# One activation for Silu, residual blocks by halves, and five changes of order in a two-layer encoder trunk

## The chip, the cores and the metric

The kernel runs on one core of a Trainium2 chip. The metric is the device time of one execution in microseconds (us), smaller being better; the median of a few runs is given with the lowest and the highest.

The engines are named as in the profile: PE (TensorE matmuls) and PEld (its weight loads), DVE (VectorE), ACT (ScalarE), POOL (GpSimd), SP (SyncE, which here only issues transfers). POOL issues transfers too.

## The reference

The input is a residual stream of 1024 tokens by 1024 features. Each of two layers computes, in float32:

```
h  = rmsnorm(x, g_mix);  p = h @ w_in
q  = rmsnorm(p[:384], g_q) @ w_uq          # 8 heads x (64 plain + 32 rotary)
kv = rmsnorm(p[384:640], g_kv) @ w_ukv     # 8 heads x (64 keys + 64 values)
k_rope = rope(p[640:672])
y_attn = softmax(q k^T / sqrt(96)) v
a, gt  = split(p[672:])
u  = a * sigmoid(gt)
u  = dwconv31(u) + b;  u = silu(layernorm(u))
x  = x + concat(y_attn, u) @ w_o
z  = dwconv3(rmsnorm(x, g_ffn) @ w_up) + b  # 2 x 2816 channels
zg, zv = split(z)
x  = x + (silu(zg) * zv) @ w_down
```

A last rmsnorm follows. silu(z) is z * sigmoid(z).

## The kernel before

Activations lie with features on the partitions and the 1024 tokens along the free axis; a block is 128 features by 1024 tokens in float32, and its halves are tokens 0 to 511 and 512 to 1023 (`HALVES`). Every matmul operand is carried as a high and a low part, both rounded to fp32r, and a product is three matmuls: high by high, high by low, low by high.

One layer goes through five stages.

**Projections** (`project`, matmuls on L210 and L479). They give the gate and value of the convolution, the query and key-value latents, the rotary parts and the queries. The gate's Sigmoid is on L532. A finished query block goes to DRAM (the spills `qd` and `qrd`), from where each head's rows are read back; the first head's rows are copied straight to its query tile `q`. The 31 taps of the convolution run on DVE (L1617) and, left over for the time of the attention, on ACT and POOL.

**Attention** (`attention`). A loop over n from -2 to 65 goes through 8 heads of 8 query tiles. One n makes the scores of tile n + 2 (six matmuls, L1438, into two PSUM banks `s`), the maximum (DVE, L1441), the exp of tile n + 1 (ACT, L1449), the transposes of tile n (L1465) with their casts `pt` on ACT (L1467) and DVE (L1468), and half of the values (L1489). `rows` (L1418) makes the values' operand for 128 tokens; `ROWS` says how many of them stand ahead of the first two scores. A table `agenda` runs further pieces after step n: the taps left over (`tap_late`, kinds `act`, `both` and `pool`: an `act` tap is one activation on L1633 and a transfer that adds it to the convolution), and the loads for the next stage. At the end `early(0, ...)` and `early(1, ...)` begin the output projection of the first two blocks.

**Output projection** (`wo_steps`, L835), with the norm of the convolution (`conv_norm`, L1652 to L1688), the residual in blocks `y`, and the second rmsnorm.

**Up projection** (`up_steps`). For each of 22 blocks f of channels seven products of half the size are made, in the order 1, 5, 6, 3, 7, 2, 4, each twelve matmuls of 128x512 (L1015). Products 1, 6, 7 and 4 go on accumulating in one bank, and 5 and 3 in another, so each of these waits until the one before it was evicted. An eviction is on ACT or on DVE (a copy or an add into `zg` or `zv`; the DVE ones on the helper line L964). The first 29 products, f from 0 to 3, have an order of their own (`START`). After them come the convolution of three taps (`o` from `zg`, `v` from `zv`; L1384 on ACT, L1390 on DVE), the Sigmoid (L1056) into a block `sg`, `gate` (o times sg) and `close` (v times o), and the store to DRAM (`act<-v`). Combined weights (`part`, `combine`, `cast`, `turn`: lines L964, L982, L1376, L1378 and L174) are made on DVE and ACT and partly added up by transfers that POOL issues.

**Down projection** (`down_steps`, L1207).

What sets the order: PE's, DVE's, ACT's and POOL's instructions keep the order in which the program writes them; SP's transfers are ordered by the framework's scheduler. In up, `put(step, rank, f)` puts a piece into the table of one step (a product is one step, 2.7 us), smaller ranks first. An eviction is put one step after its product at rank 0, unless `EVICT` names another step. The blocks share 31 buffers, so one is free again only when its last reader is done.

Of the kernel before, what the change touches and what calls it, by code (L numbers as in the profile page):

```python
# [16 lines left out]
T = 1024  # L17
# [45 lines left out]
LAST_MULT = (60, 61)  # L63
ROWS = (2, 4)
E = mybir.EngineType
# [10 lines left out]
LEFT = 4  # L76
# [8 lines left out]
ENDS = (slice(512, 768), slice(768, T))  # L85
EVICT = {(5, 0): 24, (5, 1): 25, (1, 2): 35, (1, 3): 36, (2, 2): 36, (2, 3): 37}
DOWN_ADDED = (2, 4)
# [23 lines left out]
class Encoder:  # L111
# [370 lines left out]
    def project(self, l, carry):  # L482
# [4 lines left out]
        gates, ckv, kvs, cq, cqs, vs, w = {}, [], [], [], [], [], {}  # L487
        heads, pending = {}, {}
        qd = [self.dp.tile([HEADS, NOPE, T], F32R, name=f"qd{l}{i}") for i in range(2)]
# [154 lines left out]
        def query_rope(i):  # L644
            p = ps[f"u{i}"]
            c, s = self.blk(f"rc{l}_{i}"), self.blk(f"rs{l}_{i}")
            nc.vector.tensor_tensor(out=c, in0=p, in1=st["cos"], op=ALU.mult)
            nc.vector.tensor_tensor(out=s, in0=p, in1=st["sin"], op=ALU.mult)
            st["rope", i] = c, s
            yield 2.44, 0.0  # L650
            if i == 0:
                return
            (c1, s1), (c2, s2) = st.pop(("rope", 0)), st.pop(("rope", 1))
            nc.vector.tensor_tensor(out=c1, in0=c1, in1=s2, op=ALU.subtract)
            nc.vector.tensor_tensor(out=c2, in0=c2, in1=s1, op=ALU.add)
            his = [self.blk(f"qr{l}_{i}", F32R) for i in range(2)]
            for hi, o in zip(his, (c1, c2)):
                nc.scalar.copy(out=hi, in_=o)
            yield 2.5, 1.0
            for i, (hi, o) in enumerate(zip(his, (c1, c2))):  # L660
                nc.vector.tensor_tensor(out=o.bitcast(F32R), in0=o, in1=hi.bitcast(F32), op=ALU.subtract)
                sp = hi, o.bitcast(F32R)
                yield 1.25, 0.0
                for p in range(2):
                    for h in range(DIRECT):
                        self.move(heads[h][0][p][NOPE + i * HALF:NOPE + (i + 1) * HALF, :],
                                  sp[p][h * HALF:(h + 1) * HALF, :])
                for p in range(2):
                    self.move(qrd[p][i].rearrange("h d t -> (h d) t"), sp[p], nc.gpsimd)

        def query(j):
# [112 lines left out]
    def layer(self, l, carry):  # L784
        with self.psum(f"mix{l}", ([f"w{i}" for i in range(3)], 1), 2):
            mixed = self.project(l, carry)
        with self.psum(f"attn{l}", 2, 4):
# [3 lines left out]
                     61: lambda: (ready.update({(1, 3): self.complete(*casts.pop(3))}), [casts.update({m: self.wo_cast(l, m, 1)}) for m in range(4, 8)])}  # L791
            begun = {"x": [], "po": {}}
            conv, ys = mixed[1], self.attention(l, *mixed, ahead, ready, begun)
# [43 lines left out]
    def wo_steps(self, l, conv, ys, w, casts, x, steps, put):  # L837
# [5 lines left out]
        def load_x():  # L843
            x.extend(self.load_y(l, m) for m in range(2, 8))

# [18 lines left out]
        def add_heads(c, m):  # L864
            xm = x[m][:, HALVES[c]]
            nc.vector.tensor_tensor(out=xm, in0=ps.pop((c, m)), in1=xm, op=ALU.add)

        def evict(c, m):
            xm = x[m][:, HALVES[c]]
            nc.vector.tensor_tensor(out=xm, in0=ps.pop((c, m)), in1=xm, op=ALU.add)  # L870
# [26 lines left out]
        def norm(c, k):  # L897
            xk = x[k][:, HALVES[c]]
            nc.vector.scalar_tensor_tensor(out=xk, in0=xk, scalar=par[:, P_GFFN + k:P_GFFN + k + 1], in1=rf[c],
                                           op0=ALU.mult, op1=ALU.mult)  # L900

        def first(k):
            norm(0, k)
            i = 1 + k // 4
            sets[i].append(self.pair(x[k][:, left], f"b{l}_{i}{k}", "m", True))

# [34 lines left out]
        put(18, 0.9, lambda: spread(1))  # L941
        b11, b12 = (lambda k, cs=cs: x[k][:, cs] for cs in HALVES)
        b21, b22 = (lambda k, cs=cs: x[k + 4][:, cs] for cs in HALVES)
        plan = ((5, 0, b11, b12, b11), (3, 4, b22, b22, None), (6, None, b11, b22, b11), (7, None, b12, b22, b12),
# [11 lines left out]
    def up_steps(self, l, steps, put):  # L956
# [95 lines left out]

        def sigmoid(f):
            z = st[f]
            z["s"] = self.blk(f"sg{l}_{f}")
            nc.scalar.activation(out=z["s"], in_=z["o"], func=AF.Sigmoid)  # L1056

        def gate(f):
            z = st[f]
            sub(z["o"], z["o"], z.pop("s"), ALU.mult)  # L1060

# [55 lines left out]
        for f in range(NF):  # L1117
# [288 lines left out]
    def attention(self, l, u, conv, away, spill, kvs, loaded, ahead, wo, begun):  # L1406
# [22 lines left out]
        def scores(n):  # L1429
# [4 lines left out]
            ps = self.wide(f"s{l}_{h}_{qt}")  # L1434
            for c in range(2):
                cs = slice(c * 512, (c + 1) * 512)
                for s, (i, j) in enumerate(((0, 0), (0, 1), (1, 0))):
                    nc.tensor.matmul(ps[:, cs], q[i][0:96, qs], k[j][0:96, cs],  # L1438
                                     start=(s == 0), stop=(s == 2))
            mx = self.cp.tile([128, 1], F32, name=f"mx{l}_{h}_{qt}", tag="mx", bufs=4)  # L1440
# [96 lines left out]
        def early_add(m):  # L1537
            xm = begun["x"][m][:, HALVES[0]]
            nc.vector.tensor_tensor(out=xm, in0=po[m], in1=xm, op=ALU.add)
# [21 lines left out]
        agenda[56].append(lambda: sums(last - 1, slice(0, 64), state[last - 1], state[last - 1]["y"], state[last - 1]["rb"]))  # L1561
        agenda[60].append(lambda: begun["x"].extend(self.load_y(l, m) for m in range(2)))
        for c, when in enumerate((60, 62)):
# [6 lines left out]
        for n in range(-2, total + 2):  # L1570
# [55 lines left out]
    def tap_late(self, l, j, t, u, y, kind):  # L1626
        lo, hi, s = self.span(t)
        p = self.blk(f"late{l}_{j}_{t}")
        if kind != "act":
            self.nc.gpsimd.tensor_tensor(out=p[:, lo:hi], in0=u[:, lo + s:hi + s],  # L1630
                                         in1=self.tap(l, j, t).broadcast_to([128, hi - lo]), op=ALU.mult)
        else:
            self.nc.scalar.activation(out=p[:, lo:hi], in_=u[:, lo + s:hi + s], func=AF.Copy, scale=self.tap(l, j, t))  # L1633
        if kind == "both":
# [10 lines left out]
    def conv_norm(self, l, conv, out, put):  # L1645
# [25 lines left out]
        def scale(j, c):  # L1671
            if (j, "z") not in st:
# [98 lines left out]
```

## Time and profile before

| | us |
|---|---|
| median of 3 runs | 2341.23 |
| lowest and highest | 2337.42, 2342.27 |
| the profiled execution | 2342.95 |
| its span | 2341.2 |

The span is that from the first to the last instruction of the profile; mean granted TensorE clock 0.995. Busy time is given by engine as a sum, a share of the span and a count of instructions. Busy shares are averages over stages of different kinds: a wait counts only where it is the last one to end in its stage. In a row of the timeline the brackets give how long the engine was idle ahead of it and which engine or transfer ended that.

### The profile page before, as it was taken

How to read it: one execution, taken by the hardware profiler on the slowest of the kernel's cores; microseconds unless marked ns; L12 is line 12 of the kernel's file. 1: busy time of each engine (PE TensorE's matmuls, PEld its weight loads, DVE VectorE, ACT ScalarE, POOL GpSimd, SP SyncE). 2: the span in 40 equal slices, each digit the busy share in tenths (PEclk: the TensorE clock that was granted, in tenths of full speed). 3: DMA queues.
4: the chain of work that ended last, by engine and by line, in shares of the span. 5: the costliest groups of instructions: out<-in, count | busy, mean ns of one | idle time of the engine just before them, and what ended most of it. 6: DMA issues, size and time to landing. Idle time of an engine off the chain costs nothing.

```text
span 2341.2 us, 31964 instructions
## 1 busy us (share of the span) xinstructions
PE 2298.8 (98%) x11256; PEld 1931.5 (83%) x11256; DVE 1787.9 (76%) x2404; ACT 1281.9 (55%) x2049; POOL 821.7 (35%) x837
## 2 busy tenths in 40 slices
PE   9999999999999999999999999999999999999997
PEld 7887899887788888888888888998877888888886
DVE  5987888768878787876559778887688787868665
ACT  5444877545755555544523467774465555555443
POOL 1222798613323323001412248964323332320032
PEclk9999999999999999999999999999999999999999
DMA  5887955936899998935968988547658999989366
GB/s 179 158 177 252 205 128 116 243 89 160 189 253 290 287 289 230 319 121 144 205 134 166 228 232 191 117 115 199 173 112 199 280 299 275 289 216 313 99 132 152
DMA packets 193969, 465.47 MB, mean 199 GB/s; under 512 B 26784, under 2 KB 34832, under 8 KB 193808
## 3 DMA queue, kind: packets, MB, share of 16 engines
q0 software_dynamic: 103712, 224.68, 46.3%
q1 hardware_dynamic: 90096, 238.74, 30.7%
q8 instruction: 89, 1.46, 0.3%
q14 instruction: 72, 0.59, 0.1%
HBM read 309.28 MB, written 80.40 MB: 166 GB/s over the span
## 4 chain that ended last, share of the span: by engine, by line
PE 78%; issue 6%; DVE 5%; DMA 4%; ACT 4%; POOL 2%; SPq 0%; POOLq 0%; ACTq 0%; DVEq 0%
PE p L1015 29%; PE pd L1207 14%; PE s L1438 6%; PE po L835 5%; PE o L1489 4%; PE t L1465 4%; PE pa L210 3%; PE pq L210 3%; PE pkv L210 2%; PE pg L210 2%; DMA w<-wu 1%; PE pg L479 1%; PE pk L210 1%; DVE wu L964 1%; PE pu L210 1%
## 5 line engine op out<-in xcount | busy, mean ns | idle before, releaser
L1015 PE MATMUL p<-b,w 128*128 128x512 f32 x3552 | 811.3, 390 | 8.8 <-DVE zg L964 3.3
L1015 PEld LDWEIGHTS p<-b,w 128*128 128x128 f32 x3552 | 666.6, 188 | 152.8 <-DVE zg L964 5.2
L1207 PE MATMUL pd<-ab,wd 128*128 128x512 f32 (+1 forms) x1920 | 422.3, 381 | 0.0
L1207 PEld LDWEIGHTS pd<-ab,wd 128*128 128x128 f32 x1920 | 350.7, 188 | 69.5 <-DVE ab L1378 0.4
L1438 PE MATMUL s<-k,q 96*128 96x512 f32 x768 | 208.9, 407 | 4.7 <-issue 1.9
L1468 DVE TENSOR_TENSOR pt<-t,pt 128x512 fp32r<-128x512 f32 x256 | 164.7, 684 | 60.8 <-ACT pt L1467 60.7
L175 POOL DMA_DIRECT2D w<-wu x96 | 84.1, 894 | 294.5 <-ACT w L174 265.2
L175 POOL DMA_DIRECT2D w<-in_w_up x116 | 100.9, 870 | 224.9 <-ACT w L174 210.7
L1467 ACT CAST pt<-t 128x512 fp32r<-128x512 f32 x256 | 137.5, 589 | 49.2 <-PE t L1465 43.1
L1630 POOL TENSOR_TENSOR late<-gate,par 128x1012 f32<-128x1012 f32 (+12 forms) x78 | 160.0, 2051 | 0.0
L1438 PEld LDWEIGHTS s<-k,q 96*128 96x128 f32 x768 | 134.8, 189 | 28.4 <-issue 3.8
L1441 DVE TENSOR_REDUCE mx<-s 128x1 f32<-128x1024 f32 x128 | 155.7, 1216 | 2.5 <-PE s L1438 2.5
L1489 PEld LDWEIGHTS o<-pt,v 128*128 128x128 f32 x1024 | 139.6, 190 | 13.7 <-issue 3.0
L1489 PE MATMUL o<-pt,v 128*128 128x256 f32 x1024 | 143.5, 283 | 2.8 <-DVE yt L1495 2.2
L964 DVE TENSOR_TENSOR zg<-p,zg 128x512 f32<-128x512 f32 x88 | 60.5, 690 | 111.5 <-PE p L1015 68.8
L1617 DVE SCALAR_TENSOR_TENSOR conv<-gate,par,conv 128x1009 f32<-128x1009 f32 (+7 forms) x112 | 142.3, 1274 | 3.6 <-ACT conv L541 1.0
L1449 ACT ACTIVATE p<-s,mx 128x1024 f32<-128x1024 f32 x128 | 144.9, 1132 | 0.0
L800 POOL DMA_DIRECT2D wd<-in_w_down x44 | 32.5, 741 | 310.9 <-PE pd L1207 308.8
L1465 PE MATMUL t<-ident,p 128*128 128x128 f32 x1024 | 133.6, 273 | 5.5 <-ACT p L1449 5.5
L1376 ACT CAST ab<-ac 128x512 fp32r<-128x512 f32 x130 | 80.1, 617 | 101.6 <-DVE ac L1142 99.1
L174 ACT ACTIVATE w<-w 128x512 fp32r<-128x512 f32 x212 | 133.5, 630 | 3.0
L1465 PEld LDWEIGHTS t<-ident,p 128*128 128x128 f32 x1024 | 114.4, 140 | 10.2 <-ACT p L1449 9.3
(2062 smaller groups left out, 4247.1 us busy)
## 6 DMA issues: line engine op xcount, KB each, us to landing
w<-in_w_up POOLq DMA_DIRECT2D x232, 256.0 KB, 6.5
wu<-in_w_up SPq DMA_DIRECT2D x88, 512.0 KB, 5.3
w<-wu POOLq DMA_DIRECT2D x96, 256.0 KB, 5.1
sd<-in_w_down SPq DMA_DIRECT2D x44, 512.0 KB, 9.8
ws<-sd SPq DMA_DIRECT2D x44, 512.0 KB, 6.3
wd<-in_w_down POOLq DMA_DIRECT2D x88, 256.0 KB, 5.3
act<-v SPq DMA_DIRECT2D x36, 512.0 KB, 5.9
ac<-act SPq DMA_DIRECT2D x72, 256.0 KB, 6.0
```

Of the source, the lines that this page charges most:

```text
L175: self.nc.gpsimd.dma_start(out=lo, in_=src, accum_op=ALU.add)
L210: nc.tensor.matmul(ps[:, HALVES[c]], w, x[:, HALVES[c]], start=(k == 0 and s == 0), stop=(k == n - 1 and s == 2))
L1015: nc.tensor.matmul(ps, w[p][:, k * 128:(k + 1) * 128], b[:, q], start=(i in (1, 5, 2) and k == 0 and t == 0), stop=(k == 3 and t == 2), sk ...
L1207: nc.tensor.matmul(ps[t, m][:, cs], w[i, j][p][:, m * 128:(m + 1) * 128], b[:, q, cs], start=(i in (1, 5, 2) and j == 0 and s == 0), stop= ...
L1438: nc.tensor.matmul(ps[:, cs], q[i][0:96, qs], k[j][0:96, cs], start=(s == 0), stop=(s == 2))
L1441: nc.vector.tensor_reduce(out=mx, in_=ps, op=ALU.max, axis=AX.X, negate=True)
L1449: nc.scalar.activation(out=p, in_=ps, func=AF.Exp, bias=mx, accum_out=st["sums"][:, qt:qt + 1])
L1465: nc.tensor.transpose(tp[:, i, :], p[:, kt * 128:(kt + 1) * 128], self.ident)
L1468: nc.vector.tensor_tensor(out=pt[1][g][:, :, qi * 128:(qi + 1) * 128], in0=tp, in1=hi.bitcast(F32), op=ALU.subtract)
L1489: nc.tensor.matmul(po, v[kt][:, h // 2, e, :], pt[s][kt // 4][:, kt % 4, :], start=(kt == 0 and s == 0), stop=(kt == 7 and s == 1))
L1617: self.nc.vector.scalar_tensor_tensor(out=y[:, lo:hi], in0=u[:, lo + s:hi + s], scalar=self.tap(l, j, t), in1=y[:, lo:hi], op0=ALU.mult, o ...
L1630: self.nc.gpsimd.tensor_tensor(out=p[:, lo:hi], in0=u[:, lo + s:hi + s], in1=self.tap(l, j, t).broadcast_to([128, hi - lo]), op=ALU.mult)
```

## The change

Seven things are changed.

1. **Silu.** The Sigmoid into `sg` and the product `gate` become one Silu activation in place, and so does the pair in the convolution's norm (there the add of the bias is in the activation). `close` of a block is put up to three steps earlier.
2. **Residual in halves.** `load_y` loads half blocks (128x512, blocks k and k + 4 of one half in a buffer) and first those of the first half.
3. **Query spills.** In `project` the spills of the queries are collected and written out after the next query.
4. **Taps on ACT** (`tap_late`, kind `act`) are two activations, one for each half, in two steps of the attention that hold no other such half; the adding transfer follows the second.
5. **Evictions in up.** `EVICT` names steps for (5,2), (5,3), (6,2), (6,3), (7,2), (7,3); its fraction is the rank.
6. **Scores** are made with the product of parts as the outer loop and the halves as the inner one.
7. **Order on PE in attention.** `ROWS` is (3, 4) for (2, 4): three `rows`, not two, ahead of the first scores, and one ahead of the second. Three of four parts of `early(1)` stand before the last values, behind `early(0)`.

The core of the diff:

```
-ROWS = (2, 4)
+ROWS = (3, 4)
...
-EVICT = {(5, 0): 24, (5, 1): 25, (1, 2): 35, (1, 3): 36, (2, 2): 36, (2, 3): 37}
+EVICT = {(5, 2): 30, (5, 3): 31, (6, 2): 38.295, (6, 3): 39.295, (7, 2): 40.295, (7, 3): 41.295, (5, 0): 24, (5, 1): 25, (1, 2): 35, (1, 3): 36, (2, 2): 36, (2, 3): 37}
...
-                for p in range(2):
-                    self.move(qrd[p][i].rearrange("h d t -> (h d) t"), sp[p], nc.gpsimd)
+                spills.extend((qrd[p][i].rearrange("h d t -> (h d) t"), sp[p]) for p in range(2))
...
-                self.move(qd[p][2 * j:2 * j + 2].rearrange("h d t -> (h d) t"), sp[p], nc.gpsimd)
+                spills.append((qd[p][2 * j:2 * j + 2].rearrange("h d t -> (h d) t"), sp[p]))
+            while j and spills:
+                self.move(*spills.pop(0), nc.gpsimd)
...
-    def load_y(self, l, m):
-        t = self.blk(f"y{l}_{m}")
-        self.nc.sync.dma_start(out=t, in_=self.xd[l][m])
-        return t
+    def load_y(self, l, x, c, k):
+        t = self.blk(f"y{l}_{c}{k}")
+        for e in range(2):
+            m = k + 4 * e
+            x[m, c] = t[:, HALVES[e]]
+            self.nc.sync.dma_start(out=x[m, c], in_=self.xd[l][m][:, HALVES[c]])
...
-        def sigmoid(f):
-            z = st[f]
-            z["s"] = self.blk(f"sg{l}_{f}")
-            nc.scalar.activation(out=z["s"], in_=z["o"], func=AF.Sigmoid)
-
-        def gate(f):
-            z = st[f]
-            sub(z["o"], z["o"], z.pop("s"), ALU.mult)
+        def silu(f):
+            o = st[f]["o"]
+            nc.scalar.activation(out=o, in_=o, func=AF.Silu)
...
-            put(EVICT.get((i, f), n + 1), 0, lambda i=i, f=f: evict(i, f))
+            m = EVICT.get((i, f), n + 1)
+            put(int(m), m % 1 * 10, lambda i=i, f=f: evict(i, f))
...
-            put(n + 3, 4, lambda f=f: sigmoid(f))
-            put(n + (7 if f >= LEFT else 5), 2.8, lambda f=f: gate(f))
+            put(n + 3, 4, lambda f=f: silu(f))
...
-            put(max(m + 3, n + (8 if f >= LEFT else 6)), 3, lambda f=f: close(f))
+            put(max(m + 3, n + 5), 3, lambda f=f: close(f))
...
-            for c in range(2):
-                cs = slice(c * 512, (c + 1) * 512)
-                for s, (i, j) in enumerate(((0, 0), (0, 1), (1, 0))):
-                    nc.tensor.matmul(ps[:, cs], q[i][0:96, qs], k[j][0:96, cs],
-                                     start=(s == 0), stop=(s == 2))
+            for s, (i, j) in enumerate(((0, 0), (0, 1), (1, 0))):
+                for cs in HALVES:
+                    nc.tensor.matmul(ps[:, cs], q[i][0:96, qs], k[j][0:96, cs], start=(s == 0), stop=(s == 2))
...
-        costs = [LATE_COST[kind] for kind in kinds]
+        costs, taken = [LATE_COST[kind] for kind in kinds], set()
         for i, (j, t) in enumerate(late):
-            agenda[int(SIDE_TIME * sum(costs[:i]) / sum(costs))].append(lambda i=i, j=j, t=t: self.tap_late(l, j, t, u[j], conv[j], kinds[i]))
+            n, steps = int(SIDE_TIME * sum(costs[:i]) / sum(costs)), self.tap_late(l, j, t, u[j], conv[j], kinds[i])
+            for e in range(2 if kinds[i] == "act" else 1):
+                while kinds[i] == "act" and n in taken:
+                    n += 1
+                if kinds[i] == "act":
+                    taken.add(n)
+                agenda[n].append(lambda steps=steps: next(steps, None))
+            if kinds[i] == "act":
+                agenda[n].append(lambda steps=steps: next(steps, None))
...
                 early(0, range(3))
+                early(1, range(3))
...
-        early(0, range(3, 4))
-        early(1, range(4))
         for m in range(2):
+            early(m, range(3, 4))
             early_add(m)
...
-        if kind != "act":
+        if kind == "act":
+            for a, b in ((lo, T // 2), (T // 2, hi)):
+                self.nc.scalar.activation(out=p[:, a:b], in_=u[:, a + s:b + s], func=AF.Copy, scale=self.tap(l, j, t))
+                yield
+        else:
             self.nc.gpsimd.tensor_tensor(out=p[:, lo:hi], in0=u[:, lo + s:hi + s],
                                          in1=self.tap(l, j, t).broadcast_to([128, hi - lo]), op=ALU.mult)
...
-            nc.scalar.activation(out=z, in_=y, func=AF.Sigmoid, bias=par[:, P_BLN + j:P_BLN + j + 1])
+            nc.scalar.activation(out=z, in_=y, func=AF.Silu, bias=par[:, P_BLN + j:P_BLN + j + 1])
...
-            y, z = conv[j][:, HALVES[c]], st[j, "z"][:, HALVES[c]]
-            nc.vector.scalar_tensor_tensor(out=z, in0=y, scalar=par[:, P_BLN + j:P_BLN + j + 1], in1=z,
-                                           op0=ALU.add, op1=ALU.mult)
-            nc.scalar.copy(out=out[j][0][:, HALVES[c]], in_=z)
+            nc.scalar.copy(out=out[j][0][:, HALVES[c]], in_=st[j, "z"][:, HALVES[c]])
```

The matmuls stay 11256 in number. On the other engines nothing is added but ten halves of taps in each layer.

More of the change, by code (lines that the diff above doesn't have):

```diff
@@ L487, in project @@
         gates, ckv, kvs, cq, cqs, vs, w = {}, [], [], [], [], [], {}
-        heads, pending = {}, {}
+        heads, pending, spills = {}, {}, []
         qd = [self.dp.tile([HEADS, NOPE, T], F32R, name=f"qd{l}{i}") for i in range(2)]
@@ L791, in layer @@
                      61: lambda: (ready.update({(1, 3): self.complete(*casts.pop(3))}), [casts.update({m: self.wo_cast(l, m, 1)}) for m in range(4, 8)])}
-            begun = {"x": [], "po": {}}
+            begun = {"x": {}, "po": {}}
             conv, ys = mixed[1], self.attention(l, *mixed, ahead, ready, begun)
@@ L843, in load_x @@
         def load_x():
-            x.extend(self.load_y(l, m) for m in range(2, 8))
+            for c in range(2):
+                for k in range(4):
+                    if (k, c) not in x:
+                        self.load_y(l, x, c, k)
         def cast(part, m):
@@ L864, in add_heads @@
         def add_heads(c, m):
-            xm = x[m][:, HALVES[c]]
+            xm = x[m, c]
             nc.vector.tensor_tensor(out=xm, in0=ps.pop((c, m)), in1=xm, op=ALU.add)
         def evict(c, m):
-            xm = x[m][:, HALVES[c]]
+            xm = x[m, c]
             nc.vector.tensor_tensor(out=xm, in0=ps.pop((c, m)), in1=xm, op=ALU.add)
@@ L897, in norm @@
         def norm(c, k):
-            xk = x[k][:, HALVES[c]]
+            xk = x[k, c]
             nc.vector.scalar_tensor_tensor(out=xk, in0=xk, scalar=par[:, P_GFFN + k:P_GFFN + k + 1], in1=rf[c],
@@ L904, in first @@
             i = 1 + k // 4
-            sets[i].append(self.pair(x[k][:, left], f"b{l}_{i}{k}", "m", True))
+            sets[i].append(self.pair(x[k, 0], f"b{l}_{i}{k}", "m", True))
         def combine(i, ks, srcs):
@@ L941, in wo_steps @@
         put(18, 0.9, lambda: spread(1))
-        b11, b12 = (lambda k, cs=cs: x[k][:, cs] for cs in HALVES)
-        b21, b22 = (lambda k, cs=cs: x[k + 4][:, cs] for cs in HALVES)
+        b11, b12 = (lambda k, c=c: x[k, c] for c in range(2))
+        b21, b22 = (lambda k, c=c: x[k + 4, c] for c in range(2))
         plan = ((5, 0, b11, b12, b11), (3, 4, b22, b22, None), (6, None, b11, b22, b11), (7, None, b12, b22, b12),
@@ L1537, in early_add @@
         def early_add(m):
-            xm = begun["x"][m][:, HALVES[0]]
+            xm = begun["x"][m, 0]
             nc.vector.tensor_tensor(out=xm, in0=po[m], in1=xm, op=ALU.add)
@@ L1561, in attention @@
         agenda[56].append(lambda: sums(last - 1, slice(0, 64), state[last - 1], state[last - 1]["y"], state[last - 1]["rb"]))
-        agenda[60].append(lambda: begun["x"].extend(self.load_y(l, m) for m in range(2)))
+        agenda[60].append(lambda: [self.load_y(l, begun["x"], 0, k) for k in range(2)])
         for c, when in enumerate((60, 62)):
@@ L1628, in tap_late @@
         p = self.blk(f"late{l}_{j}_{t}")
-        if kind != "act":
+        if kind == "act":
[3 more added lines that the diff above has]
+        else:
             self.nc.gpsimd.tensor_tensor(out=p[:, lo:hi], in0=u[:, lo + s:hi + s],
                                          in1=self.tap(l, j, t).broadcast_to([128, hi - lo]), op=ALU.mult)
-        else:
-            self.nc.scalar.activation(out=p[:, lo:hi], in_=u[:, lo + s:hi + s], func=AF.Copy, scale=self.tap(l, j, t))
         if kind == "both":
```

## The prediction

> **What bounds the kernel now.** I read the page's first part, then the list of waits for TensorE (PE), because where one engine is nearly always busy only its idle time can be won. The two lines of the page, and then the waits (columns: total us, times, longest us):
>
> ```profile
> span 2341.2 us, 31964 instructions
> PE 2298.8 (98%) x11256; PEld 1931.5 (83%) x11256; DVE 1787.9 (76%) x2404; ACT 1281.9 (55%) x2049; POOL 821.7 (35%) x837
> ...
> PE t L1465 <- ACT p L1449: 5.5, 14, 0.5
> PE p L1015 <- DVE zg L964: 3.3, 2, 1.8
> PE p L1015 <- ACT zv L1026: 2.4, 4, 0.8
> PE o L1489 <- DVE yt L1495: 2.2, 2, 1.1
> PE p L1015 <- DVE zv L964: 2.0, 1, 2.0
> PE s L1438 <- issue: 1.9, 1, 1.9
> ...
> PE o L1489 <- DVE pt L1468: 0.6, 2, 0.3
> ```
>
> PE is idle for 2341.2 - 2298.8 = 42.4 us. The seven waits quoted add up to 17.9 us, and two more for the first query, shown below, to 2.4. The change touches what ends most of these and nothing else on PE, whose 11256 matmuls stay. So a gain is at most some 20 us, plus what idle time costs indirectly. The row by stretch shows that (columns: us, busy of PE, PEld, DVE, ACT, POOL, PEclk, DMA share, GB/s):
>
> ```profile
> 200.00:250.00 50.00, 46.79 (x246) 39.08 (x246) 38.24 (x52) 30.88 (x58) 25.30 (x27) 0.97 0.87 245
> ...
> 1760.00:1790.00 30.00, 28.01 (x116) 22.54 (x116) 27.16 (x29) 17.31 (x24) 8.76 (x12) 0.94 0.81 214
> 1790.00:2200.00 410.00, 410.00 (x1811) 339.49 (x1810) 315.38 (x401) 221.50 (x346) 96.66 (x129) 1.00 0.92 259
> ```
>
> In the long stretch of up and down of layer 2 PE is never idle, so whatever is taken from DVE, ACT or POOL there is worth nothing. Two stretches hold a stall of about 2 us and also a granted clock below 1: 0.03 x 50 = 1.5 us and 0.06 x 30 = 1.8 us at full speed are lost with it.
>
> **The change, part by part.** *Start of attention.* The first score group of each layer waits for the query's high half, and after two matmuls again for its low half:
>
> ```profile
> 207.75 0.61 PE L210 MATMUL pn<-cqs_2l,wu10h 128*128 128x512 f32 x2
> 208.20 0.62 PE L210 MATMUL pn<-cqs_2h,wu10l 128*128 128x512 f32 x2
> ...
> 211.84 0.70 PE L1438 MATMUL s<-k,q 96*128 96x512 f32 x2 [0.30 <-DVE conv L1617]
> 214.46 1.46 PE L1438 MATMUL s<-k,q 96*128 96x512 f32 x4 [1.92 <-issue]
> ...
> 1365.35 0.70 PE L1438 MATMUL s<-k,q 96*128 96x512 f32 x2 [1.34 <-DMA q<-qrd]
> 1367.15 1.16 PE L1438 MATMUL s<-k,q 96*128 96x512 f32 x4 [1.10 <-DMA q<-qn]
> ```
>
> A 128x512 matmul takes 0.45/2 = 0.225 us (two per 0.45 us). ROWS puts one more `rows` (6 matmuls) ahead of the scores, and the new order of scores runs four matmuls, not two, before the low half: 8 x 0.225 = 1.8 us of work moved into waits of 2.2 us and 2.4 us, so 1.8 per layer, 3.6 together. The query lands as before: the spills keep their place in POOL's queue and SP's order is unchanged, so that edit counts nothing. The bounds are 0 (the next wait, for the first exp, takes it all) and 4.6, all of these waits. In layer 1 the stall that is left is 0.30 + 1.92 - 1.8 = 0.4 us, far from one that cost clock, so I also take the 1.5 us. Elsewhere the other order of 768 score matmuls counts nothing: the pairs pn above alternate between halves with one weight, and run at full rate.
>
> [...]
>
> *Taps on ACT in halves.* Step time and ACT's work (start, us; then groups: count, busy us, mean ns):
>
> ```profile
> 239.35 1.62 PE L1438 MATMUL s<-k,q 96*128 96x512 f32 x6
> ...
> 242.56 0.71 PE L1438 MATMUL s<-k,q 96*128 96x512 f32 x2
> ...
> L1449 ACT ACTIVATE p<-s,mx 128x1024 f32<-128x1024 f32 x128 | 144.9, 1132 | 0.0
> L1449 ACT ACTIVATION_READ_ACCUMULATOR p<-s,mx 128x1 f32 x128 | 27.1, 211 | 0.0
> L1467 ACT CAST pt<-t 128x512 fp32r<-128x512 f32 x256 | 137.5, 589 | 49.2 <-PE t L1465 43.1
> L1633 ACT ACTIVATE late<-gate,par 128x1019 f32<-128x1019 f32 x4 | 4.7, 1177 | 0.0
> L174 ACT ACTIVATE w<-w 128x512 fp32r<-128x512 f32 x212 | 133.5, 630 | 3.0
> ...
> L174 ACT ACTIVATE wc_2l<-wc_2h 128x1024 fp32r<-128x1024 f32 x2 | 2.1, 1062 | 5.3 <-DMA wc_2h<-in_w_up 5.3
> ```
>
> A step is 242.56 - 239.35 = 3.21 us. With a whole tap ACT has 1.132 + 0.211 + 2 x 0.589 + 1.177 = 3.70 us in it, 0.49 too much: that is the longest of the 14 waits on p (0.5), 5.5 us in all. Splitting costs 2 x 630 - 1062 = 198 ns by the rows of L174, so a half is near (1.177 + 0.2)/2 = 0.69, and the step holds 3.21 us, just what there is. Steps with a tap are twice as many, though, and none has slack. Bounds: -5.5 (all waits go) and +4.0 (20 x 0.198, all on the path). I take -3, nearer to the first, since the overrun itself is gone. POOL's accumulating transfer follows the second half; taps on ACT lie in the first half of attention, so no sum at its end waits for it.
>
> [...]
>
> *End of attention.* The last values wait, in each layer, for yt and pt:
>
> ```profile
> 437.57 0.35 PE L1489 MATMUL o<-pt,v 128*128 128x256 f32 x1 [1.12 <-DVE yt L1495]
> 438.20 2.06 PE L1489 MATMUL o<-pt,v 128*128 128x256 f32 x15 [0.28 <-DVE pt L1468]
> ```
>
> Nine matmuls of `early(1)` (9 x 0.225 = 2.0 us) now stand ahead of them and cover 1.12 + 0.28 = 1.4 us per layer: -2.8. Bounds 0 (the norm's sums behind are late instead) and -2.8; I take the latter, as what they read was cast long before.
>
> *Evictions.* In each layer product (7,2) waits some 1.7 us for the eviction of (6,2) on DVE (3.3 in all), which stood behind the gate and other work:
>
> ```profile
> 599.66 1.22 DVE L964 TENSOR_TENSOR o<-o,sg 128x1024 f32<-128x1024 f32 x1
> ...
> 602.59 0.69 DVE L964 TENSOR_TENSOR zg<-p,zg 128x512 f32<-128x512 f32 x1
> ```
>
> The gate is gone and EVICT puts the eviction ahead of what stood between, so it can run up to 602.59 - 599.66 = 2.9 us earlier: this wait goes. Late next is (7,3), behind the eviction of (6,3), which follows a weight pair whose cast ACT does not finish earlier. I take 1.2 per layer, -2.4, between 0 and -3.3. The four waits on zv (ACT, 2.4 us) are served sooner by (5,2) and (5,3), but a weight block that lands as before is late next: 0, bound -2.4.
>
> *Silu.* These leave DVE, or change function on ACT:
>
> ```profile
> L1056 ACT ACTIVATE sg<-o 128x1024 f32<-128x1024 f32 x44 | 46.4, 1055 | 5.6 <-DVE o L1390 5.1 <-DMA ws<-sd 0.5
> L964 DVE TENSOR_TENSOR o<-o,sg 128x1024 f32<-128x1024 f32 x44 | 53.5, 1217 | 0.0
> L532 ACT ACT_TABLE_LOAD x3 | 3.8, 1283 | 0.1
> ```
>
> DVE is relieved of 53.5 us and of 16 products of the convolution's norm; ACT keeps its count at the same elements. The program has one table load more, 1.283 us, at layer 2's first gate in the projection, where PE has matmuls queued: 0, bound +1.3. The 53.5 us lie beside a PE that is never idle, but in layer 2's start they count at one place. There ACT waited for a store before it could reuse a block, DVE ran late behind it, and PE stood:
>
> ```profile
> 1777.60 1.24 ACT L1384 ACTIVATE v<-zv,par 128x1024 f32<-128x1024 f32 x1 [2.39 <-DMA act<-v]
> ...
> 1784.00 0.68 DVE L964 TENSOR_TENSOR zv<-p,zv 128x512 f32<-128x512 f32 x1
> ...
> 1784.74 1.64 PE L1015 MATMUL p<-b,w 128*128 128x512 f32 x4 [1.99 <-DVE zv L964]
> ```
>
> Without sg fewer blocks are held, `close` and its store go up to three steps earlier, and this activation has another block. The stall of 2.0 and the clock's 1.8 make 3.8; I take -3, bounds 0 and -3.8.
>
> *Residual in half blocks* has the same bytes, elements and SP place: 0.
>
> The sum: 3.6 + 1.5 + 3.0 + 2.8 + 2.4 + 3.0 = 16.3 us. The profiled execution took 2342.95 us (span 2341.2 and 1.75 around it), 1.7 above the median 2341.23. So 2342.95 - 16.3 = 2326.7 there, and **2325.0** as a median. With every wait gone: 4.6 + 1.5 + 5.5 + 2.8 + 5.7 + 3.8 = 23.9, 2317.3.
>
> **The rivals.** (1) *Absorbed.* What PE does earlier meets waits that don't move with it: landing transfers above all (DMA share 0.81 to 0.92 in the rows above). Then the start of attention (3.6) and half of the other 11.2 without the clock remain, 9.2, or less if the start too is eaten: 4 to 9 us, 2332 to 2337. For it: three of the nine waits name a transfer or issue. Against: most name an engine whose order the change alters. (2) *The clock stays low* in the two windows, though the stalls are shorter: 1.5 of the sum falls away, and 1.4 of the 3.0 (as 1.8 of 3.8): 2328. [...] Against: both windows hold the largest stalls. (3) *Slower.* `close` now stands on DVE directly ahead of the eviction that product (4) waits for, for 18 blocks in each layer (f from 4 to 21):
>
> ```profile
> 722.51 0.69 DVE L964 TENSOR_TENSOR wu<-wu,wu 128x512 f32<-128x512 f32 x1
> ...
> 723.85 0.69 DVE L964 TENSOR_TENSOR zv<-p,zv 128x512 f32<-128x512 f32 x1 [0.65 <-PE p L1015]
> ...
> 726.57 0.69 DVE L964 TENSOR_TENSOR zg<-p,zg 128x512 f32<-128x512 f32 x1 [0.83 <-PE p L1015]
> ```
>
> DVE is free at 723.20; a `close` of 1.22 us (as the gate's row) ends at 724.42, the eviction at 725.11, and (4) starts when the product before it ends, by 726.57: 1.4 us to spare. If Silu or the last tap holds `close` by more than that, each excess counts 36 times: at 2 us late 0.6 x 36 = 22, so 2347. Against: the Sigmoid that Silu replaces ran steps before this point.
>
> **How the numbers follow.** Forecast as summed 0.6, absorbed 0.2, clock 0.1, slower 0.1. The range: from 2317.3, every wait gone, up to 2337, the end of the absorbed case; outside are the slower rival (0.1), and about 0.1 for what is more or less than these bounds. A measurement of this kernel can tell about 0.2%, 4.7 us, from no change: 2336.5 is the edge. The absorbed case lies half on either side: faster 0.6 + 0.1 + 0.1 = 0.8, same 0.1, slower 0.1.
>
> **What would show it.** In the changed kernel's waits for PE: p L1449 at 2.5 us or less; the lines on zg, yt and pt gone or under 1 us; zv on DVE gone; the granted clock 1.00 in both stretches, the first score group at most 1 us late. DVE near 1787.9 - 53.5 = 1734 us busy or a little less, PE's idle time down from 42.4 to some 29. I would be wrong if these waits went and the span did not follow (then the first rival), or if p <- zv on DVE grew with tens of counts (the third).

## The result and the profile after

The changed kernel took 2323.06 us (median of 6 runs, 2321.58 to 2324.69), the kernel before beside it 2341.75 us (6 runs, 2337.42 to 2345.32): a ratio of 0.9922, 95% interval 0.9909 to 0.9934. Forecast were 2325.0 us and a range of 2317 to 2337. The kernel before, run again with each set of experiments, had medians of 2339.34, 2338.11 and 2338.84 us (15, 8 and 25 runs), so the gain may be nearer to 16 us than to the 18.7 between the two medians here.

The page of the changed kernel:

```profile
span 2321.4 us, 31847 instructions
PE 2293.4 (99%) x11256; PEld 1929.9 (83%) x11256; DVE 1726.9 (74%) x2344; ACT 1286.4 (55%) x2070; POOL 823.2 (35%) x837
```

The span is 19.8 us shorter. PE's idle time fell from 42.4 to 2321.4 - 2293.4 = 28.0 us, and its busy time by 5.4 us, although it runs the same matmuls: 3.4 of that are two stretches at half clock that are gone (from 215.15 and from 1785.28 us in the kernel before, with a granted clock of 0.50). DVE lost 61.0 us. The list of waits of PE, the lines that answer to those shown of before:

```profile
PE p L1021 <- DMA w<-in_w_up: 2.3, 2, 1.4
...
PE p L1021 <- ACT zv L1032: 1.3, 2, 0.9
PE s L1438 <- issue: 1.2, 1, 1.2
...
PE s L1438 <- DMA q<-qn: 0.8, 1, 0.8
PE t L1464 <- ACT p L1448: 0.8, 2, 0.4
...
PE p L1021 <- DVE zg L970: 0.6, 1, 0.6
```

The waits on yt, pt and zv (by DVE) are gone; those on p, zg, zv (by ACT) and the query are smaller. One is new at this size, a weight block by transfer, 2.3 us where before it was 0.9. By stretch:

```profile
200.00:250.00 50.00, 48.52 (x272) 41.23 (x271) 40.49 (x57) 35.09 (x68) 26.46 (x26) 1.00 0.91 256
1750.00:1780.00 30.00, 30.00 (x134) 24.82 (x133) 24.83 (x26) 20.21 (x29) 10.18 (x14) 1.00 0.93 232
1780.00:2200.00 420.00, 420.00 (x1854) 347.77 (x1854) 304.57 (x403) 224.15 (x351) 92.45 (x123) 1.00 0.88 253
```

Both places of low clock are at 1.00. The start of up in layer 2, where PE stood for 2.0 us, has no idle time; and in the long stretch, where PE was never idle before, DVE's relief shows only as DVE busy for less (304.57 of 420 us; before 315.38 of 410).

Starts of the same matmul in the two traces, subtracted, say where the 19.8 us came from. To the end of the projections 1.3 us (no gain of the change: 0.6 at a first weight and 0.7 at 168 us, where the kernel before waits for `kvs_1l`; E10, whose first projections are those of before, does not wait there either); start of attention with the clock 3.2; the rest of layer 1's attention 0.4; its end 2.0; up's start 1.5; from there to layer 2's attention 0.6; layer 2's start 2.0, its attention 0.7, its end 1.9, up's start 3.0 and the stall with half clock behind it 3.6; 0.5 is given back after that.

### The profile page after: what moved, and what is told of

It reads as the page before. It is cut to its first block, busy times and chain, and to the rows that moved or that the text cites. A ratio compares the mean times of both kernels' runs of the same rounds, so it can differ in the third digit from the quotient of the medians.

```text
span 2321.4 us, 31847 instructions
## 1 busy us (share of the span) xinstructions
PE 2293.4 (99%) x11256; PEld 1929.9 (83%) x11256; DVE 1726.9 (74%) x2344; ACT 1286.4 (55%) x2070; POOL 823.2 (35%) x837
## 4 chain that ended last, share of the span: by engine, by line
PE 81%; DVE 5%; DMA 5%; ACT 4%; issue 4%; POOL 1%; SPq 0%; POOLq 0%; ACTq 0%; DVEq 0%
PE p L1021 30%; PE pd L1208 18%; PE po L838 6%; PE s L1438 6%; PE o L1488 4%; PE t L1464 4%; PE pa L210 2%; PE pg L210 2%; DVE conv L1624 2%; DMA w<-wu 2%; PE pq L210 1%; PE pg L479 1%; PE pkv L210 1%; ACT p L1448 1%; ACT pt L1466 1%
## 5 line engine op out<-in xcount | busy, mean ns | idle before, releaser
L1391 DVE SCALAR_TENSOR_TENSOR o<-zg,par,o 128x1023 f32<-128x1023 f32 x88 | 112.7, 1283 | 79.3 <-ACT o L1385 77.9
```

## The experiments

E10 is the kernel before with one part of the change, E12 has two edits, and each of the others is the changed kernel with one edit. Their medians are set against 2323.06 us; executions of one kernel lie 2 to 8 us apart and the medians are of 4 to 11 runs, so 1 to 2 us of that comparison are not to be trusted, and each reading also rests on the wait that the edit was to bring back.

**E1, taps on ACT whole.**

```
-            for a, b in ((lo, T // 2), (T // 2, hi)):
-                self.nc.scalar.activation(out=p[:, a:b], in_=u[:, a + s:b + s], func=AF.Copy, scale=self.tap(l, j, t))
-                yield
+            self.nc.scalar.activation(out=p[:, lo:hi], in_=u[:, lo + s:hi + s], func=AF.Copy, scale=self.tap(l, j, t))
+            yield
...
```

> The changed kernel with the 20 ACT taps whole again, one step each; all else as changed. Theory (the listed waits are the loss): PE t <- ACT p goes back from 0.8 to 5.5 us and the time by 4.7, to 2327.8. Rival (the list leaves out many short delays that the halves brought, some 0.23 us each at every second half; in the changed kernel's trace they add up to 4.5 us, where the whole taps cost 6.7): the time goes up by only 2.1, to 2325.2.

Measured: 2324.28 us (5 runs, 2322.63 to 2325.32), 1.2 more. The list of waits of E1, then the groups of ACT in the changed kernel:

```profile
PE t L1464 <- ACT p L1448: 5.6, 14, 0.5
```

```profile
L1638 ACT ACTIVATE late<-gate,par 128x512 f32<-128x512 f32 x20 | 14.6, 729 | 0.2
...
L1638 ACT ACTIVATE late<-gate,par 128x507 f32<-128x507 f32 x4 | 2.9, 721 | 0.0
```

The listed wait is back by 4.8 us, and the time by 1.2. The starts of the matmuls show the rest: in the changed kernel ten transposes in each layer begin 0.13 to 0.30 us late, mostly at every second step, 4.5 us in all, of which the list, which counts idle time by modelled ends, names 0.8. In E1 the same delays add up to 6.7 us. The rival holds, at its lower end.

**E2, the old EVICT table.**

```
-EVICT = {(5, 2): 30, (5, 3): 31, (6, 2): 38.295, ..., (7, 3): 41.295, (5, 0): 24, ...
+EVICT = {(5, 0): 24, ...
```

> The changed kernel with the old EVICT table. Theory (the evictions' place took the waits on zg away): the waits of (7,2), 1.7 us in each layer, come back in full or less what the absent gate gives, 2.4 to 3.3 us in all: 2325.5 to 2326.4. Rival (the gate's absence alone moved the eviction early enough): no change within 0.5 us, 2323.

Measured: 2326.16 us (5 runs, 2325.34 to 2327.14), 3.1 more. The list of waits of E2:

```profile
PE p L1021 <- DVE zg L970: 3.8, 4, 1.1
PE p L1021 <- ACT zv L1032: 3.1, 4, 0.8
```

Both waits are back, so the steps named for the evictions took them away, not the gate's absence. The theory holds, at the upper end.

**E3, Silu undone in up.**

```
...
-            put(n + 3, 4, lambda f=f: silu(f))
+            put(n + 3, 4, lambda f=f: sigmoid(f))
+            put(n + (7 if f >= LEFT else 5), 2.8, lambda f=f: gate(f))
...
-            put(max(m + 3, n + 5), 3, lambda f=f: close(f))
+            put(max(m + 3, n + (8 if f >= LEFT else 6)), 3, lambda f=f: close(f))
```

> The changed kernel with Sigmoid into sg, the gate's product on DVE and close at its old step, in up; the convolution's norm keeps Silu. Theory (Silu took away layer 2's stall of 2 us with its half clock, 3.6 us between 1754 and 1789 us of the first trace, and part of the waits on zg): 3 to 6 us slower, 2326 to 2329, with the granted clock below 1 again in layer 2's start of up. Rival (the evictions alone removed that stall, Silu is hidden under a busy PE): 2323 to 2324.

Measured: 2337.43 us (11 runs, 2334.58 to 2340.42), 14.4 more; its ratio to the kernel before is 0.9994 (0.9984 to 1.0004), so nearly nothing of the change is left. The timeline of E3, first in layer 1 and then in layer 2, and its stretches:

```profile
606.88 1.22 DVE L970 TENSOR_TENSOR v<-v,o 128x1024 f32<-128x1024 f32 x1
...
610.56 0.33 SPq L974 DMA_DIRECT2D wu<-in_w_up  x1
610.99 0.85 SPq L1074 DMA_DIRECT2D act<-v  x2
...
616.36 1.24 ACT L1391 ACTIVATE v<-zv,par 128x1024 f32<-128x1024 f32 x1 [1.66 <-DMA act<-v]
...
618.64 1.72 PE L1021 MATMUL p<-b,w 128*128 128x512 f32 x6 [2.11 <-ACT zv L1032]
...
1769.57 1.24 ACT L1391 ACTIVATE v<-zv,par 128x1024 f32<-128x1024 f32 x1 [4.36 <-DMA act<-v]
...
1771.85 3.36 PE L1021 MATMUL p<-b,w 128*128 128x512 f32 x7 [4.78 <-ACT zv L1032]
```

```profile
600.00:640.00 40.00, 37.89 (x159) 30.84 (x160) 36.63 (x38) 24.62 (x36) 13.55 (x20) 0.96 0.81 204
1750.00:1790.00 40.00, 34.80 (x141) 28.23 (x142) 33.09 (x35) 21.74 (x31) 11.09 (x15) 0.91 0.74 182
```

The stall comes back, in both layers now and up to 4.78 us long: ACT waits until a store has landed before it may write v, the eviction behind it waits, then PE, and the granted clock of the two stretches is 0.96 and 0.91 (0.04 x 40 + 0.09 x 40 = 5.2 us). The kind of stall is as forecast, but 14.4 us are far over the 3 to 6 expected.

The order of SP's transfers (SPq is the queue in which SP issues them) shows why the store is late. Those of the changed kernel, with the `close` of that block:

```profile
600.23 0.33 SPq L974 DMA_DIRECT2D wu<-in_w_up  x1
...
603.67 1.22 DVE L970 TENSOR_TENSOR v<-v,o 128x1024 f32<-128x1024 f32 x1
...
604.91 0.33 SPq L1069 DMA_DIRECT2D act<-v  x1
...
609.08 0.33 SPq L974 DMA_DIRECT2D wu<-in_w_up  x1
```

Here the first store of a block leaves as soon as `close` has ended (604.89). In E3 the scheduler put the second weight load ahead of it; that load waits 7.8 us for a transfer (`w<-wu`) before it starts at 610.56, and the store leaves 2.9 us after `close` has ended (608.10), in layer 2 4.3 us after it. Without these delays the activation's waits, 1.66 and 4.36 us, would be nearly gone (an estimate from these rows). The kernel before, E4, E9 and E10 have the order load, store, load, store; only E3 has both loads first. So a part of the 14.4 us comes from what the scheduler made of this edit, and is not the worth of Silu itself.

**E4, close late.**

```
-            put(max(m + 3, n + 5), 3, lambda f=f: close(f))
+            put(max(m + 3, n + (8 if f >= LEFT else 6)), 3, lambda f=f: close(f))
```

> The changed kernel with Silu, but close and its store at their old steps, up to three later. Theory (sg blocks were what the activation at 1777.6 us lacked, so Silu in place is enough): no change, 2323. Rival (the store was the wait: act <- v must land before its block is used again, and it is now late as before): the stall of 2.0 us and the half clock in layer 2 come back, 2326 to 2327.

Measured: 2323.70 us (5 runs, 2322.34 to 2326.07), no change. This says nothing of a late `close` at the place of the stall, though: in E4's trace the edit moves only later blocks, and the first store still leaves 4.68 us after the weight load before it, as in the changed kernel.

**E9, Silu into a block of its own.**

```
-            o = st[f]["o"]
-            nc.scalar.activation(out=o, in_=o, func=AF.Silu)
+            z = st[f]
+            z["s"] = self.blk(f"sg{l}_{f}")
+            nc.scalar.activation(out=z["s"], in_=z["o"], func=AF.Silu)
...
-            sub(z["v"], z["v"], z["o"], ALU.mult)
+            sub(z["v"], z["v"], z["s"], ALU.mult)
```

> The changed kernel, but Silu writes a block of its own (sg) instead of working in place, and close multiplies by that; no gate, close at its new step. DVE is as in the changed kernel, the blocks are allocated as in the kernel before. Theory (blocks: the 31 buffers go round once more per f, so an activation gets a buffer whose store has not landed): stalls of 2 us or more at v <- zv with act <- v as releaser come back in up's start of both layers, 5 to 14 us slower, 2328 to 2337. Rival (DVE's 54 us for the gate were what made the start late): 2323 within 1 us.

Measured: 2325.28 us (4 runs, 2323.23 to 2325.61), 2.2 more: between the two. The list of waits of E9:

```profile
PE p L1021 <- ACT zv L1032: 2.3, 3, 0.8
...
PE p L1021 <- DVE zv L970: 1.2, 2, 0.8
```

These two waits grow by 2.2 us together, none of them is over 0.8, and no activation waits for a store. So the extra block alone makes no big stall. E3 has the gate on DVE and the late `close` besides. Which of them led to the order of SP's transfers stays open: the gate needs its block, so its time by itself could not be separated, and the block with the late `close` but no gate wasn't tried.

**E10, the kernel before with Silu alone** (in up and in the convolution's norm, close at its new step):

```
-            put(n + 3, 4, lambda f=f: sigmoid(f))
-            put(n + (7 if f >= LEFT else 5), 2.8, lambda f=f: gate(f))
+            put(n + 3, 4, lambda f=f: silu(f))
...
-            put(max(m + 3, n + (8 if f >= LEFT else 6)), 3, lambda f=f: close(f))
+            put(max(m + 3, n + 5), 3, lambda f=f: close(f))
...
-            nc.scalar.activation(out=z, in_=y, func=AF.Sigmoid, bias=par[:, P_BLN + j:P_BLN + j + 1])
+            nc.scalar.activation(out=z, in_=y, func=AF.Silu, bias=par[:, P_BLN + j:P_BLN + j + 1])
...
```

> The kernel before with Silu alone, in up and in the convolution's norm, and close at its new step. Theory of the prediction (the parts add up): layer 2's stall with its half clock goes, 3.6 us, and part of the waits on zg, 1 us: 4 to 5 us faster than before, 0.998. Rival (as taking Silu out of the changed kernel cost 14 us, it is the main part by itself): 10 us or more faster, 0.995 or less.

Measured: 2337.62 us (10 runs, 2334.59 to 2341.08) beside 2338.84 for before; ratio 0.9995 (0.9986 to 1.0005). Neither the theory nor the rival. The stretch with the stall, before and then E10, which has one more row, the start of attention in layer 2:

```profile
1740.00:1800.00 60.00, 55.88 (x235) 44.65 (x234) 49.89 (x55) 39.05 (x57) 19.69 (x28) 0.97 0.81 192
```

```profile
1740.00:1800.00 60.00, 58.74 (x258) 47.82 (x257) 48.39 (x55) 38.41 (x57) 19.03 (x27) 1.00 0.87 211
1340.00:1380.00 40.00, 37.99 (x168) 30.75 (x166) 28.35 (x37) 18.46 (x32) 8.44 (x15) 0.96 0.80 269
```

In the trace the stall and its half clock are gone, as forecast: 23 more matmuls get into the same 60 us. But a lower clock stands at layer 2's start of attention instead (0.96 over 40 us, some 1.6 us; the profiled execution of before had 1.00 there), and the medians show no gain. The profiled execution of before, 2342.95 us, is also 4.1 us above the median beside E10, so its trace may show more than its executions lose as a rule. Silu alone gives about nothing (E10), all the rest without Silu in up gives about nothing (E3), both together 0.9922.

**E5, ROWS = (2, 4).**

```
-ROWS = (3, 4)
+ROWS = (2, 4)
```

> The changed kernel with ROWS = (2, 4). Theory: six matmuls, 1.36 us in each layer, come after the query's wait again: 2.7 us slower, and in layer 1 the stall is 1.37 + 1.36 us, so the half clock comes back and adds 1.5: 2327.3. Rival (the clock follows where a stall lies, not this one): 2325.8 with the clock at 1.00 from 200 to 250 us.

Measured: 2325.16 us (5 runs, 2321.40 to 2328.05), 2.1 more. The waits and stretches of E5, whose profiled execution is the slowest of the five:

```profile
PE s L1438 <- issue: 1.6, 1, 1.6
PE s L1438 <- DMA q<-qn: 1.2, 1, 1.2
```

```profile
205.00:240.00 35.00, 32.91 (x171) 27.16 (x170) 27.62 (x41) 22.74 (x47) 13.46 (x12) 0.95 0.80 251
1340.00:1380.00 40.00, 38.22 (x177) 31.02 (x176) 29.34 (x40) 22.56 (x41) 12.45 (x17) 0.96 0.81 249
```

Both starts of attention have a lower clock in that execution (0.95 over 35 us and 0.96 over 40 us: 1.75 and 1.6 us), and that execution is 2.9 us slower than the median of the five. The same stretches of other traces agree: of the six starts of attention with two `rows` ahead (before, E5, E10) four have a clock of 0.95 or 0.96 and two of 1.00, and the twelve with three or four `rows` (changed kernel, E2, E3, E9, E11, E12) all have 1.00. So with the rows moved ahead the clock stays up in these traces, and without them it is lower in some executions and not in others.

**E6, halves as the outer loop of the scores.**

```
-            for s, (i, j) in enumerate(((0, 0), (0, 1), (1, 0))):
-                for cs in HALVES:
+            for cs in HALVES:
+                for s, (i, j) in enumerate(((0, 0), (0, 1), (1, 0))):
```

> The changed kernel with halves as the outer loop of the scores. Theory: only the first group of each layer counts, two matmuls less ahead of the low half's wait: 2 x 0.45 = 0.9 us slower, 2324.0. Rival (768 score matmuls run differently in this order): 2 us or more either way, seen in the step of 3.21 us.

Measured: 2322.60 us (5 runs, 2321.55 to 2323.80), 0.5 less: no effect that can be told. The 0.45 us per layer that I gave to this order isn't shown by this run; nor is any harm.

**E7, early(1) behind the last values.**

```
                 early(0, range(3))
-                early(1, range(3))
...
-            early(m, range(3, 4))
+            early(m, range(4) if m else range(3, 4))
```

> The changed kernel with early(1, ...) behind the last values as before. Theory: the waits on yt and pt come back, 1.4 us in each layer by the list of waits and 1.8 to 2.0 by the starts of the matmuls: 2325.9 to 2327.0. Rival (what follows was late anyway): less than 1 us.

Measured: 2326.41 us (5 runs, 2324.62 to 2327.45), 3.4 more. The timeline of the changed kernel, then that of E7:

```profile
433.25 2.08 PE L1488 MATMUL o<-pt,v 128*128 128x256 f32 x16
```

```profile
427.79 0.39 PE L838 MATMUL po_e<-ys_5h,wo 128*128 128x512 f32 x1
429.32 0.35 PE L1488 MATMUL o<-pt,v 128*128 128x256 f32 x1 [1.14 <-DVE yt L1494]
429.95 2.06 PE L1488 MATMUL o<-pt,v 128*128 128x256 f32 x15 [0.28 <-DVE pt L1467]
```

In the changed kernel the sixteen values run without a gap. In E7 the listed idle is 1.42 us, while the starts lie 1.53 us apart (427.79 to 429.32) where 0.23 is due, and 0.63 where 0.12 is: 1.8 us lost in each layer, 3.6 in both. The listed idle is the smaller of the two measures again.

**E8, spills and residual as before** (the loads of whole blocks, the spills at once):

```
-        t = self.blk(f"y{l}_{c}{k}")
-        for e in range(2):
-            m = k + 4 * e
-            x[m, c] = t[:, HALVES[e]]
-            self.nc.sync.dma_start(out=x[m, c], in_=self.xd[l][m][:, HALVES[c]])
+        t = self.blk(f"y{l}_{m}")
+        self.nc.sync.dma_start(out=t, in_=self.xd[l][m])
+        return t
...
-                spills.extend((qrd[p][i].rearrange("h d t -> (h d) t"), sp[p]) for p in range(2))
+                for p in range(2):
+                    self.move(qrd[p][i].rearrange("h d t -> (h d) t"), sp[p], nc.gpsimd)
...
```

> The changed kernel with the query's spills and the residual's loads as before. Theory: both were forecast at nothing; 2323 within 1 us. Rival (the half blocks bring the first half of the residual earlier and take a wait in the output projection or its norm away): 1 to 2 us slower.

Measured: 2326.64 us (5 runs, 2323.60 to 2328.95), 3.6 more. The timeline of the changed kernel at an eviction of product 5 on ACT, then E8 there and in the output projection:

```profile
569.22 0.58 ACT L1032 COPY zv<-p 128x512 f32<-128x512 f32 x1
```

```profile
443.48 0.50 PE L837 MATMUL po<-ys_1h,wo 128*128 128x512 f32 x1 [0.38 <-DMA wo<-in_w_o]
...
573.99 0.59 ACT L1028 COPY zv<-p 128x512 f32<-128x512 f32 x1 [4.69 <-DVE y L912]
...
577.14 1.31 PE L1017 MATMUL p<-b,w 128*128 128x512 f32 x3 [0.82 <-ACT w L1373]
```

With whole residual blocks the eviction waits 4.69 us for the last reader of a block y, the casts behind it on ACT are late, and PE waits for one of them, in both layers; a weight of the output projection also lands later. The changed kernel has no such wait. So by these rows the residual's blocks are what lets the early eviction of (5, 2) run. At the first scores the wait for the query is listed at 1.0 and 1.1 us in E8 and 1.2 and 0.8 in the changed kernel, and it varies with the execution (0.6 and 0.4 in E4, 0.7 and 0.7 in E7, with the same order there): nothing speaks for the spills, though they were not undone alone.

**E11 and E12, a version that might beat both.** E11 keeps the halves of taps out of two steps in a row; E12 also has ROWS = (4, 4).

```
-                    taken.add(n)
+                    taken.update((n - 1, n, n + 1))
```

> The changed kernel with the halves of the ACT taps never in two steps in a row. Theory (one half fits a step, the second in a row is what delays the transposes, by some 0.23 us, ten times in each layer): those delays go, 4.5 us faster than the changed kernel, 2318.6. Rival (the halves that go later collide with other work, or POOL waits for them with its own taps behind): no gain, 2323 or more.

> As the kernel with the halves apart, and ROWS = (4, 4): all four rows ahead of the first scores. Theory: the low half's wait that is left, 1.37 and 1.01 us in the changed kernel's trace, is covered by 1.36 us of matmuls: another 2.0 to 2.4 us, 2316.4. Rival (the first exp is then late, since the second scores follow the first at once and nothing stands between them for PE to do): no gain or up to 1 us slower than with the halves apart alone.

Measured: E11 2333.54 us (10 runs, 2330.08 to 2338.34), 10.5 more; E12 2332.79 us (10 runs, 2329.43 to 2335.06). Neither beats the changed kernel. The list of waits of E11, and its timeline on ACT and POOL:

```profile
PE t L1464 <- ACT p L1448: 13.5, 6, 8.9
```

```profile
414.66 2.31 POOL L1644 TENSOR_TENSOR conv<-conv,late 128x1009 f32<-128x1009 f32 x1 [4.14 <-DMA conv<-late]
416.93 2.34 POOL L1515 TENSOR_TENSOR yt<-yt,rb 128x1024 f32<-128x1024 f32 x1
...
419.30 1.04 ACT L193 CAST ys_5h<-yt 128x1024 fp32r<-128x1024 f32 x1 [8.46 <-POOL yt L1515]
```

The short delays are gone: by the starts of the matmuls no transpose of E11 from 220 to 310 us and from 1375 to 1470 us begins over 0.02 us late. In their place POOL, which keeps its order and waits for each adding transfer, comes to the attention output (L1515) at 416.93, where the changed kernel has it at 408.24; ACT stands behind it for 8.46 us, and PE for 8.9. Two shorter waits for p come before it (1.4 us of delay at 316 us, 2.4 at 370), and the mean clock from 240 to 430 us is 0.96. All this is in layer 1; in layer 2 the halves apart are faster than the changed kernel's by 1.8 us from start to end of the attention. The rival holds. In E12 the first scores wait for nothing, and twelve of them run in one piece:

```profile
210.75 2.91 PE L1438 MATMUL s<-k,q 96*128 96x512 f32 x12
```

The exp is not late either: between 206 and 232 us the starts in E12 lose 0.3 us, in E11 1.5. So ROWS = (4, 4) does in the trace what was expected, while the medians of E12 and E11 differ by 0.75 us only; with the taps left as they are it wasn't tried.

## Why the prediction was right, step by step

*The limit.* Idle time of PE and its clock were all there was to gain, and both fell about as summed: idle to 28.0 us, where "some 29" stood; DVE to 1726.9, where 1734 or less stood.

*Start of attention, 3.6 and 1.5 us.* By the starts 5.2 us in both layers, the clock among them, where 5.1 were forecast; by the list the waits fell from 4.6 to 2.0. That the clock stays up with the moved rows fits E5 and the traces named there (1.00 in twelve starts of twelve). The part given to the order of scores (0.9) isn't shown (E6), and one sign was missed: the first scores are still 1.2 us late in layer 1, not 1 at most.

*Taps, 3.0 us.* Too large: 2.2 by the delays of E1 against those of the changed kernel, 1.2 by E1's median, and 1.1 between the two kernels over the attention behind its start. The step that failed is the cost of a split, 198 ns from weight casts. A half takes 0.721 to 0.729 us, so a pair costs about 1.45 - 1.16 = 0.29 us more than a whole, and a step 1.13 + 0.21 + 2 x 0.589 + 0.73 = 3.25 us, more than the 3.21 it has. The list of waits, from which I took 5.5 as all there was, made the gain look larger still.

*End of attention, 2.8 us.* Right in kind, too small: 3.9 between the two kernels by the starts (2.0 and 1.9), 3.6 in E7 by the starts and 3.4 by its median.

*Evictions, 2.4 us.* E2 gives 3.1, within its bounds.

*Silu, 3.0 us.* The stall and its clock went, 3.6 us by the starts. But the term is not one that can be added: taken out of the changed kernel Silu costs 14.4 us (E3, with a store held up in SP's queue), and put into the kernel before it is worth about nothing by the medians (E10). The forecast could come out because each of its terms was priced with all the other edits in place.

*Residual, 0.* The wrong term. "Same bytes, elements and SP place" overlooked which buffer the next eviction takes over. E8 gives 3.6 us, for it and the spills together; its rows show only the residual's part.

*The sum.* 16.3 us forecast, 18.7 between the medians and 19.8 between the two profiled executions. That the sum fits so well is partly luck. The taps were 1 to 2 us too large; the end of attention was 1 too small, up's start about 2 (4.5 us by the starts, for evictions and residual, where 2.4 were forecast), and 1.3 us lie in projections that differ from one execution to the next. The costs of undoing single parts add up to 1.2 + 3.1 + 14.4 + 2.1 - 0.5 + 3.4 + 3.6 = 27.3 us, more than the whole gain: the parts hold each other up, and E3's part is more than half of it.

*The rivals.* Absorbed: only a little; the wait for a weight by transfer grew from 0.9 to 2.3 us, at product (4, 0), which stands next in line behind the evictions. Clock stays low: no, 1.00 in both places. Slower, `close` ahead of the eviction: no, the wait on zv by DVE is gone.

## What to carry to other kernels

A list of idle time is not a list of losses: compare when the same instructions start in two traces, as twenty delays of some 0.2 us, 4.5 in all, stood in the list as 0.8, and 3.6 us as 2.8. Where buffers go round in a ring, an edit that changes the order or life of a block can move a wait to another place, and a part that is worth nothing by itself (E10) can cost most of the gain when it is taken out (E3): price the whole, undo parts one by one before calling one of them the cause, and look at the order of the transfers too, since a scheduler may have changed it with the edit. Work spread more evenly over one engine (E11) moves its followers, too; look who stands behind each queue before stretching it.

## What the runs showed of the hardware that was not expected

A stall of about 2 us has a lower granted clock beside it in one trace and not in another. The starts of attention in layer 1 and layer 2, of the kernel before and then of E10:

```profile
205.00:240.00 35.00, 32.30 (x160) 26.33 (x159) 27.52 (x40) 20.94 (x42) 12.95 (x13) 0.95 0.89 280
1340.00:1380.00 40.00, 37.55 (x172) 30.61 (x172) 29.35 (x36) 16.36 (x29) 7.26 (x13) 1.00 0.87 297
```

```profile
205.00:240.00 35.00, 32.13 (x175) 26.62 (x174) 28.16 (x42) 23.92 (x47) 15.64 (x15) 1.00 0.86 260
1340.00:1380.00 40.00, 37.99 (x168) 30.75 (x166) 28.35 (x37) 18.46 (x32) 8.44 (x15) 0.96 0.80 269
```

PE is idle for 2.70 and 2.87 us in the two stretches of layer 1, and its list of waits names one of 1.9 us at the first scores in both traces; the clock is 0.95 in one and 1.00 in the other. In layer 2, with 2.45 and 2.01 us idle, it is the other way round, 1.00 and 0.96. What decides between them isn't shown by these runs.

The same piece of work can differ between executions. From 160 to 205 us, in the kernel before, the changed kernel and E11 (one row of each):

```profile
160.00:205.00 45.00, 43.67 (x189) 35.63 (x188) 33.48 (x37) 18.42 (x20) 9.54 (x14) 0.92 0.83 211
```

```profile
160.00:205.00 45.00, 44.14 (x192) 36.29 (x192) 34.68 (x38) 17.36 (x20) 8.93 (x13) 0.92 0.83 219
```

```profile
160.00:205.00 45.00, 44.03 (x206) 36.18 (x204) 37.38 (x40) 18.55 (x20) 9.73 (x15) 1.00 0.90 242
```

0.08 x 45 = 3.6 us lie between the clock of one execution and another, in a stretch whose matmuls no edit changes: as much as most of the effects here, and a reason to read them from the trace besides the medians. In the changed kernel the clock is 0.50 from 172.49 to 179.31 us; what lowers it there wasn't tested.
